# Feed forward of an encoder layer in pools left open from the second phase, with halves of whole token tiles and rows loaded part by part

## The chip, the core and the metric

The kernel runs on one core of one Trainium2 chip. The metric is the device time of one execution in microseconds (us), the median over several runs. Engines are named PE (TensorE: matmul; PEld is its weight load), DVE (VectorE), ACT (ScalarE), POOL (GpSimd) and SP (SyncE, which issues the DMAs here).

## The reference

One layer of a streaming encoder on 1024 prompt tokens and 8 × 16 = 128 sample tokens, model width 1024. All of it is computed in float32 accuracy:

```python
hq, hf, hi, hg, aq, ak, av = split_in(yp @ w_in)
mix = concat([hgrn(hq, hf, hi, hg), window_attention(aq, ak, av)]) @ w_out
mk, mv = mem_kv(mem_prompt, w_mem_kv)
x = layer_norm(ALPHA * x + mix)
x = layer_norm(ALPHA * x + mem_attention(x, mk, mv, w_mem_q, w_mem_o))
x = layer_norm(ALPHA * x + (silu(x @ w_g) * (x @ w_u)) @ w_ffn_out)
```

The sample tokens go through the same with their own caches. The change concerns the last line, called the feed forward below, whose hidden width is 2816 (22 tiles of 128, 11 pairs of tiles).

## The kernel before, in words

**Precision.** An operand in float32 is split in two: hi is a cast to fp32r (ACT, L138), lo the rest (DVE, L139); a product is three matmuls, hi·hi, lo·hi and hi·lo (all at L96). A weight tile arrives by a DMA of 512 KB into one of three raw buffers (w_raw, L149), and its halves stand in w_hi and w_lo.

**Stages.** Phase 1, to about 463 us: the combined projection, the recurrence, window attention, and the keys and values of the memory, whose copies (ACT, L269) and stores (SP, L270, L272) end it. Phase 2, 472 to 861 us: w_out, attention to the memory and its output weights, with layer norms; the rows x2 that it makes go to DRAM (x_scratch). Then the feed forward in three stages.

**Fill stage, 861 to 920 us.** The first product of the feed forward uses Strassen's form: a 2 × 2 split of weights and of x2 with seven products in place of eight. all_operands makes the seven operands of the x2 side: for each of eight token tiles, eight transposes through TensorE (L100), copies out of PSUM (ACT, L928), four subtractions (POOL, L935), seven casts (ACT, L939) and seven lo halves (DVE, one on POOL, L940). The 64 first and 64 last tokens of a tile are the two halves e. Beside it runs filler(): the gate and up products of five pairs for the 128 sample tokens, in plain float32, with weights loaded for it (L973), two sums of the PSUM bank b, and sample_gated (L961 to L964).

**Hidden stage, 920 to 1403 us.** hidden(i) makes one of 11 pairs: four weight tiles a11, a21, a22, a12 (L1004), three sums s1, s2, s4 of them (POOL, L1011 to L1013), seven products of 24 matmuls; the results are combined to m0 and m1, gated into th (L1030 to L1032), combined on POOL to the operands of the second product (t1, t2, T3 at L1067 to L1069, t4 at L1077), and stored in h_scratch (L1036). Pairs not done in the fill stage also make the sample's part (sample_pair).

**Second projection, 1403 to 1735 us.** The pairs are taken in five parts (0,2), (2,4), (4,6), (6,8), (8,11). A part multiplies the operands of two token blocks (0,1), then the sample's, then blocks (2,3); for each of seven steps operand() loads hq from h_scratch (L1161), casts hh (ACT, L1162) and takes hl (DVE or POOL, L1163). Sums go from PSUM to the rows y by add() (DVE, L1174; some through a copy and POOL, L1171 and L1172). The weights of a pair are loaded as raw2 (L1118), summed by four subtractions on POOL (L1121 to L1124), cast (ACT, L1131) and split (L1132) in prepare(i). All rows y are loaded first, as 16 DMAs of 64 rows (L1087), which take x2 back as ALPHA·x. The sample's operands hs are loaded in sample() (L1210), one buffer each. At the end final_norm writes the output, two DMAs per half row (L1089).

**What sets the order.** Each engine works through its instructions in the order in which they were written into the program; a small planner (Order) interleaves the generators by estimated TensorE time and by rank. SP's DMAs are in the same order as well, and a DMA whose buffer isn't free holds all behind it. Pools are regions of memory: closing one and opening another makes the new tiles wait for the last users of the old ones. Before, the weight pool wp is closed and opened again after phase 1, and closed with p2 before the hidden stage, where a pool f1 takes its place.

Of the kernel before, what the change touches and what calls it, by code (L numbers as in the profile page):

```python
# [9 lines left out]
F32 = mybir.dt.float32  # L10
# [23 lines left out]
FILL = 5  # L34
# [68 lines left out]
def trunk(ctx, tc, I, O):  # L103
# [12 lines left out]
    first = ctx.enter_context(ExitStack())  # L116
    cp = first.enter_context(tc.tile_pool(name="cp", bufs=1))
# [104 lines left out]
    tri = cp.tile([P, 640], U8, name="tri")  # L222
    own = cp.tile([P, 8], F32, name="own")
    sinks = cp.tile([P, 8], F32, name="sinks")
    sinks_s = cp.tile([P, 2], F32, name="sinks_s")
    gnorm = cp.tile([P, P], F32, name="gnorm")
# [3 lines left out]
    carry = cp.tile([P, HGH, P], F32, name="carry")  # L230
    V.memset(carry, 0.0)
    starts = [cp.tile([P, GW], F32, name=f"starts{i}") for i in range(2)]
# [672 lines left out]

# [16 lines left out]
    def operands(ops, j, row):  # L922

        b = {}
        st = big("stage").rearrange("p (q k e c) -> p q k e c", q=2, k=4, e=2)
        for q in range(2):
            ps = transposes(row[:, q * 512:q * 512 + 512])
            S.copy(st[:, q], ps.rearrange("p (k e c) -> p k e c", k=4, e=2))  # L928
            for e in range(2):
                b[f"B{q + 1}{e + 1}"] = st[:, q, :, e]  # L930
        tt = big("tt").rearrange("p (a k c) -> p a k c", a=4, k=4)
        for n in range(4):
            b[f"T{n + 1}"] = tt[:, n]
        for o, x, y in (("T1", "B12", "B11"), ("T2", "B22", "T1"), ("T3", "B22", "B12"), ("T4", "B21", "T2")):
            G.tensor_tensor(b[o], b[x], b[y], op=ALU.subtract)  # L935
        c = slice(j * 64, j * 64 + 64)
        for o in OPS:
            hi, lo = ops[o]
            S.copy(hi[:, :, c], b[o])  # L939
            (G if o == "T4" else V).tensor_tensor(lo[:, :, c], b[o], hi[:, :, c].bitcast(F32), op=ALU.subtract)  # L940

    def all_operands(ops, rows, ready):
        got = list(rows)

        def load(j):
            got.insert(j, big("x2_row"))
            nc.sync.dma_start(out=got[j], in_=x2_dram[TILES[j]])

        load(0)
        load(1)  # L950
        yield 3500.0
        for j in range(8):
            operands(ops, j, got[j])
            if j < 3:
                load(j + 2)
            yield 3300.0
        order.set(ready, 2000.0)
# [8 lines left out]
    def filler():  # L966

        for i in range(FILL):
            ps = [bank("b")[:, :256] for _ in range(2)]
            for e in range(2):  # L970
                for q in range(2):
                    w = raw_tile()
                    nc.sync.dma_start(out=w, in_=I["w_f1"][i, e * 2 + q])  # L973
                    for z in range(2):
                        for kt in range(4):
                            T.matmul(ps[z][:, cols(e)], w[:, cols(z * 4 + kt)], xs[:, q * 4 + kt],
                                     start=q == kt == 0, stop=q == 1 and kt == 3)
                    yield
            h = big("h_s")[:, :256].rearrange("p (e t) -> p e t", e=2)
            sample_gated(i, h, [x.rearrange("p (e t) -> p e t", e=2) for x in ps])  # L980
            yield

# [16 lines left out]
    def hidden(f1, ops, i, then):  # L999

        def wt(name, j=None):
            t = f1.tile([P, 1024], F32, name=name, tag="w", bufs=8)
            if j is not None:
                nc.sync.dma_start(out=t, in_=I["w_f1"][i, j])  # L1004
            return t

        th = [f1.tile([P, 1024], F32, name="th", bufs=2) for _ in range(2)]
        t1, t2 = (f1.tile([P, 512], F32, name=x) for x in ("t1", "t2"))
# [5 lines left out]
        m0 = [f1.tile([P, 1024], F32, name="m0", bufs=2) for _ in range(2)]  # L1014
        m1 = [f1.tile([P, 512], F32, name="m1", bufs=2) for _ in range(2)]
        t4 = f1.tile([P, 512], F32, name="t4")
# [64 lines left out]
    def out_rows(dst, b, e, row, store):  # L1081

        for n in range(2):
            at = dst[TILES[2 * b + n]][e * 64:e * 64 + 64]
            r = row[n * 64:n * 64 + 64]
            if store is None:
                nc.sync.dma_start(out=r, in_=at)  # L1087
            else:
                nc.sync.dma_start(out=at[:, store], in_=r[:, store])  # L1089

    def final_norm(y, gb, st, b, e):
# [11 lines left out]
        for hs in (h1, h0):  # L1103
            if e is None:
                nc.sync.dma_start(out=O["y"][SAMPLE][:, hs], in_=y[:, hs])
            else:
                out_rows(O["y"], b, e, y, hs)
# [42 lines left out]
    def second_projection(f2, c, ahead, prepared, prepare):  # L1150
# [54 lines left out]
        def sample(part, first, last):  # L1205
            ws = [prepared[i] for i in range(*part)]
            k = len(ws)
            for n, wk in enumerate(ws):
                q, hi, lo = (f2.tile([P, 2, P], t, name=x) for x, t in (("hs", F32), ("hsh", F32R), ("hsl", F32R)))
                nc.sync.dma_start(out=q, in_=hs_dram[:, part[0] + n])  # L1210
                split(q, hi, lo)
                for half in range(2):
                    for x in range(2):
                        mm3(sums[half], cut((hi, lo), ALL, x), wk[f"A{half + 1}{x + 1}"],
# [3 lines left out]
        prepare(PARTS[0][1], f2)  # L1218
# [3 lines left out]
        for e in range(2):  # L1222
            for b in range(4):
                out_rows(x2_dram, b, e, y[b, e], None)
        for n, part in enumerate(PARTS):
            last = n == len(PARTS) - 1
            if last:
# [5 lines left out]
            yield from sample(part, n == 0, last)  # L1233
            if last:
# [3 lines left out]
                for half in range(2):  # L1238
                    c = slice(half * 512, half * 512 + 512)
                    V.scalar_tensor_tensor(ys[:, c], ys[:, c], ALPHA, sums[half], op0=ALU.mult, op1=ALU.add)  # L1240
                    V.bn_stats(bn[:, half], ys[:, c])
# [3 lines left out]
                return  # L1245
            yield from blocks(part, (2, 3), gb)
            for _ in range(*part):
                if len(prepared) < PAIRS:
                    i = len(prepared)
                    prepare(i, f2 if i % 2 else None)  # L1250

    def feed_forward(rows):
# [3 lines left out]
        ready = Event()  # L1256
        order.add(all_operands(ops, rows, ready), 6)
        order.add(filler(), 10)
# [13 lines left out]
        for i in range(PAIRS):  # L1272
            yield from hidden(f1, ops, i, ahead if i == PAIRS - 1 else nop)
        fs.close()
# [193 lines left out]
```

## Time and profile before

| | |
|---|---|
| time, median of 3 runs | 1737.71 us (1733.31 to 1739.44) |
| the profiled execution | 1736.8 us, span 1734.9 us |
| PE busy | 1628.2 us, 94% |
| DVE, ACT, POOL busy | 1124.7, 679.9, 496.5 us |
| mean granted clock of TensorE | 0.973 |
| longest waits of PE | 22.1 us to 1425.0, 8.9 to 472.4, 5.7 to 920.1 |

A row of the waits names the engine and tile that waited, the instruction that came last, the sum, the count and the longest. A row of the timeline has start, length, engine, line, operation and count, and in brackets the idle time before and what ended it. SPq is SP's queue: its length is the time that issuing took. Granted clock 1.00 is the full clock.

### The profile page before, as it was taken

Reading aid. Unit: us, or ns where it says so; the run is one execution under the profiler, and the core shown is the slowest. Engines: PE = TensorE matmul, PEld = TensorE weight load, DVE = VectorE, ACT = ScalarE, POOL = GpSimd, SP = SyncE. Lnnn points to the kernel's source line nnn. Section 1 sums busy time; section 2 is a strip of 40 time slices with the busy share of each in tenths; the row PEclk is TensorE's granted clock in tenths of the full one; section 3 lists DMA queues with packets and bytes.
Section 4 is the critical chain, followed back from the end, with each engine's and each line's share of the span. In section 5 each row is a group of like instructions: output and inputs, shape, how many; then the busy total and the mean of one; then the engine's idle time right before and its main releaser. Section 6 shows DMA issues by size and latency. Waiting matters only on the chain.

```text
span 1734.9 us, 24529 instructions
## 1 busy us (share of the span) xinstructions
PE 1628.2 (94%) x9065; PEld 1400.6 (81%) x9065; DVE 1124.7 (65%) x2045; ACT 679.9 (39%) x1393; POOL 496.5 (29%) x401
## 2 busy tenths in 40 slices
PE   8999999999799999999978999999999948889896
PEld 7998999999688987889876888888888746667675
DVE  6886788778477666786676555444444745767576
ACT  4543456456433544225263333322222423333421
POOL 1111121111000000100075343333323535576555
PEclk9999999999999999999999999999999979999998
DMA  7453353344964588555373333322222283233353
GB/s 234 133 169 118 98 157 96 96 126 143 302 224 166 180 269 292 194 165 200 112 253 115 106 104 117 104 82 73 78 86 78 88 231 128 80 114 111 103 142 98
DMA packets 115320, 250.02 MB, mean 144 GB/s; under 512 B 12288, under 2 KB 58496, under 8 KB 115200
## 3 DMA queue, kind: packets, MB, share of 16 engines
q1 hardware_dynamic: 115200, 248.46, 44.5%
q8 instruction: 71, 1.16, 0.3%
q14 instruction: 49, 0.40, 0.1%
HBM read 205.75 MB, written 42.60 MB: 143 GB/s over the span
## 4 chain that ended last, share of the span: by engine, by line
PE 75%; DMA 8%; POOL 6%; DVE 6%; ACT 2%; issue 2%; SPq 1%; POOLq 0%; ACTq 0%; DVEq 0%
PE a L96 47%; PE b L96 20%; DMA hq<-h_scratch 3%; PE b L100 3%; PE x L96 2%; PE z L96 2%; POOL hl L1163 1%; PE s L96 1%; DVE w L1132 1%; DMA raw<-in_w_f_dram 1%; DMA y<-x_scratch 1%; DMA w_raw<-in_w_f_dram 1%; POOL s L1124 1%; DMA w_raw<-in_w_mv_dram 1%; POOL s L1123 1%
## 5 line engine op out<-in xcount | busy, mean ns | idle before, releaser
L139 DVE TENSOR_TENSOR w_lo<-w_raw,w_hi 128x1024 fp32r<-128x1024 f32 (+1 forms) x169 | 205.1, 1216 | 121.3 <-ACT w_hi L138 120.6
L138 ACT CAST w_hi<-w_raw 128x1024 fp32r<-128x1024 f32 (+1 forms) x169 | 174.6, 1035 | 200.7 <-PE a L96 82.8
L96 PE MATMUL a<-w_hi,q_hi 128*128 128x256 f32 (+1 forms) x576 | 198.9, 346 | 8.9 <-ACT w_hi L138 8.9
L96 PE MATMUL a<-w_lo,q_hi 128*128 128x256 f32 (+1 forms) x576 | 197.3, 343 | 0.0
L96 PE MATMUL a<-w_hi,q_lo 128*128 128x256 f32 (+1 forms) x576 | 196.1, 340 | 0.0
L96 PE MATMUL a<-q_hi,w_hi 128*128 128x384 f32 x528 | 187.2, 355 | 7.1 <-ACT q_hi L138 4.3
L96 PE MATMUL a<-q_lo,w_hi 128*128 128x384 f32 x528 | 180.7, 343 | 0.2 <-DVE q_lo L139 0.2
L96 PE MATMUL a<-q_hi,w_lo 128*128 128x384 f32 x528 | 180.7, 343 | 0.0
L96 PE MATMUL x<-w,hh 128*128 128x512 f32 x344 | 112.3, 408 | 40.2 <-ACT hh L1162 22.5
L96 PEld LDWEIGHTS a<-w_hi,q_hi 128*128 128x128 f32 x576 | 109.2, 190 | 22.7 <-ACT w_hi L138 9.3
L96 PEld LDWEIGHTS a<-w_lo,q_hi 128*128 128x128 f32 x576 | 109.4, 190 | 14.3 <-issue 1.2
L96 PEld LDWEIGHTS a<-w_hi,q_lo 128*128 128x128 f32 x576 | 109.3, 190 | 13.1 <-issue 0.5
L139 DVE TENSOR_TENSOR w_lo<-a,w_hi 128x1024 fp32r<-128x1024 f32 x43 | 58.4, 1359 | 88.6 <-ACT w_hi L138 88.6
L96 PEld LDWEIGHTS x<-w,hh 128*128 128x128 f32 x344 | 66.1, 195 | 59.9 <-ACT hh L1162 23.3
L96 PEld LDWEIGHTS a<-q_hi,w_hi 128*128 128x128 f32 x528 | 100.6, 190 | 12.0 <-ACT q_hi L138 4.5
L698 POOL TENSOR_TENSOR rs<-rs,mhalf 128x1 f32<-128x1 f32 x18 | 17.2, 958 | 312.6 <-DVE rs L697 312.6
L96 PE MATMUL a<-T_h,w_hi 128*128 128x512 f32 x264 | 104.3, 395 | 0.7 <-DVE m L1060 0.7
L96 PE MATMUL a<-T_h,w_lo 128*128 128x512 f32 x264 | 104.2, 395 | 0.0
L96 PE MATMUL a<-T_l,w_hi 128*128 128x512 f32 x264 | 104.2, 395 | 0.0
L96 PEld LDWEIGHTS a<-q_lo,w_hi 128*128 128x128 f32 x528 | 100.5, 190 | 2.3 <-DVE q_lo L139 1.3
L96 PEld LDWEIGHTS a<-q_hi,w_lo 128*128 128x128 f32 x528 | 100.6, 190 | 0.8 <-DVE w_lo L139 0.4
L1162 ACT CAST hh<-hq 128x512 fp32r<-128x512 f32 (+2 forms) x75 | 46.3, 619 | 106.6 <-DMA hq<-h_scratch 75.7
(305 smaller groups left out, 3957.7 us busy)
## 6 DMA issues: line engine op xcount, KB each, us to landing
a<-in_w_f_dram SPq DMA_DIRECT2D x44, 512.0 KB, 4.0
w_raw<-in_w_fm_dram SPq DMA_DIRECT2D x41, 512.0 KB, 4.1
hq<-h_scratch SPq DMA_DIRECT2D x54, 256.0 KB, 2.7
w_raw<-in_w_tm_dram SPq DMA_DIRECT2D x24, 512.0 KB, 3.5
w_raw<-in_w_out_dram SPq DMA_DIRECT2D x24, 512.0 KB, 4.8
w_raw<-in_w_mq_dram SPq DMA_DIRECT2D x24, 512.0 KB, 4.3
w_raw<-in_w_mo_dram SPq DMA_DIRECT2D x24, 512.0 KB, 4.0
h_scratch<-th SPq DMA_DIRECT2D x44, 256.0 KB, 2.2
```

Source lines behind the costliest of these rows:

```text
L96: return self.eng.matmul(out, lhsT, rhs, **kw)
L100: return self.eng.transpose(out, in_, identity)
L138: S.copy(hi, src)
L139: V.tensor_tensor(lo, src, hi.bitcast(F32), op=ALU.subtract)
L698: G.tensor_tensor(rs, rs, mhalf[:, 0:1], op=ALU.pow)
L1123: G.tensor_tensor(s4, a12, s2, op=ALU.subtract)
L1124: G.tensor_tensor(s3, a11, a21, op=ALU.subtract)
L1132: (G if name in ("A21", "A22") else V).tensor_tensor(lo, src, hi.bitcast(F32), op=ALU.subtract)
L1162: S.copy(hi, q)
L1163: (G if o in ("T1", "T3", "T4") else V).tensor_tensor(lo, q, hi.bitcast(F32), op=ALU.subtract)
```

## The change

It does the following.

1. The small constants and the recurrence's state go to the constant pool, and the state's memory (both) later serves as xs and hs. So the weight pool wp (three raw, four hi and four lo buffers) stays open from phase 1 through the hidden stage, and phase 2's pool (tiles of big(), ten buffers) through the hidden stage too.
2. FILL is 4 in place of 5, so that one more pair makes its sample's part in the hidden stage; the filler's sums are in bank a; the hidden stage waits for the filler's event.
3. operands() works on two whole token tiles j and j + 4 at a time, as halves e: four steps with tiles of 128x512, in place of eight steps with 128x256. All five rows that must be loaded are loaded first.
4. hidden() takes its tiles from big() and raw_tile(); t1 and t2 lie in m0's upper halves, t4 in m1[0].
5. The second projection's y rows are whole tiles, one DMA of 512 KB each; four are loaded ahead of the first part, four behind its blocks (0,1). The output is one DMA per half row. sample_operands loads and casts hs of all pairs of a part, in two buffers each, ahead of sample(). prepare(i) stands around sample() and blocks (2,3), and no longer behind both.

```diff
-FILL = 5
+FILL = 4
...
+            for e in range(2):
+                ps = transposes(rows[e][:, q * 512:q * 512 + 512])
+                S.copy(st[:, e], ps.rearrange("p (k c) -> p k c", k=4))
+                b[f"B{q + 1}{e + 1}"] = st[:, e]
...
-        for j in range(8):
-            operands(ops, j, got[j])
-            if j < 3:
-                load(j + 2)
-            yield 3300.0
-        order.set(ready, 2000.0)
+        for j in range(4):
+            operands(ops, j, (got[j], got[j + 4]))
+            yield 6000.0
+        order.set(ready, 1000.0)
...
-            ps = [bank("b")[:, :256] for _ in range(2)]
+            ps = [bank("a")[:, :256] for _ in range(2)]
...
+        th = [raw_tile() for _ in range(2)]
+        m1 = raw_tile()
...
+        m0 = [big("m0") for _ in range(2)]
+        t1, t2, t4 = m0[0][:, 512:], m0[1][:, 512:], m1[0]
...
-            pair = parts_of(w, *(f1.tile([P, 1024], F32R, name=x, bufs=3) for x in ("w_hi", "w_lo")))
+            pair = parts_of(w, *(wp.tile([P, 1024], F32R, name=x, bufs=N_W) for x in ("w_hi", "w_lo")))
...
+        def sample_operands(part):
+            out = []
+            for i in range(*part):
+                q, hi, lo = (f2.tile([P, 2, P], t, name=x, bufs=2) for x, t in (("hs", F32), ("hsh", F32R), ("hsl", F32R)))
+                nc.sync.dma_start(out=q, in_=hs_dram[:, i])
+                split(q, hi, lo)
+                out.append((hi, lo))
+            return out
...
-        prepare(PARTS[0][1], f2)
+        def more():
+            i = len(prepared)
+            if i < PAIRS:
+                prepare(i, f2 if i % 2 else None)
...
-        for e in range(2):
-            for b in range(4):
-                out_rows(x2_dram, b, e, y[b, e], None)
...
+            if n == 0:
+                for e in range(2):
+                    for b in range(2):
+                        nc.sync.dma_start(out=y[b, e], in_=x2_dram[TILES[b + 4 * e]])
...
             yield from blocks(part, (0, 1), gb)
-            yield from sample(part, n == 0, last)
+            hs = sample_operands(part)
+            if n == 0:
+                for e in range(2):
+                    for b in range(2, 4):
+                        nc.sync.dma_start(out=y[b, e], in_=x2_dram[TILES[b + 4 * e]])
+            while len(prepared) < min(part[1] + 1, PAIRS):
+                more()
+            yield from sample(part, hs, n == 0, last)
...
+            while len(prepared) < PARTS[n + 1][1]:
+                more()
             yield from blocks(part, (2, 3), gb)
-            for _ in range(*part):
-                if len(prepared) < PAIRS:
-                    i = len(prepared)
-                    prepare(i, f2 if i % 2 else None)
...
-        left.close()
-        fs = ExitStack()
-        f1 = fs.enter_context(tc.tile_pool(name="f1", bufs=1, reuse_waits="tile"))
+        yield filled
...
-    first.close()
-    left.close()
-    xp = ctx.enter_context(tc.tile_pool(name="xp", bufs=1, reuse_waits="tile"))
-    xs, hs = xp.tile([P, KT, P], F32, name="xs"), xp.tile([P, 256], F32, name="hs")
-    wp = left.enter_context(tc.tile_pool(name="wp", bufs=1, reuse_waits="tile"))
```

Three places in the order of the instructions. The first is SP between phases 1 and 2, before: in_w_mv are the value weights of the memory, in_w_out the first weights of phase 2, raw the operands of phase 2, kv_sb the keys and values that phase 1 stores.

```order
L149 DMA w_raw<-in_w_mv_dram 128x1024 x2
L205 DMA raw<-mix_scratch 128x384 x2
L270 DMA out_dram<-kv_sb 128x512
L272 DMA mem_kv_scratch<-kv_sb 128x256 x2
L270 DMA out_dram<-kv_sb 128x512
L272 DMA mem_kv_scratch<-kv_sb 128x256 x2
L720 DMA rows<-in_xtok_dram 128x1024 x3
L690 DMA ln_gb<-in_ln_dram 128x1024 x2
L270 DMA out_dram<-kv_sb 128x512
L272 DMA mem_kv_scratch<-kv_sb 128x256 x2
L270 DMA out_dram<-kv_sb 128x512
L149 DMA w_raw<-in_w_out_dram 128x1024 x3
```

And the same place of SP's order now:

```order
L147 DMA w_raw<-in_w_mv_dram 128x1024 x2
L147 DMA w_raw<-in_w_out_dram 128x1024
L203 DMA raw<-mix_scratch 128x384 x2
L271 DMA out_dram<-kv_sb 128x512
L273 DMA mem_kv_scratch<-kv_sb 128x256 x2
L271 DMA out_dram<-kv_sb 128x512
L273 DMA mem_kv_scratch<-kv_sb 128x256 x2
L147 DMA w_raw<-in_w_out_dram 128x1024
L721 DMA rows<-in_xtok_dram 128x1024 x3
L147 DMA w_raw<-in_w_out_dram 128x1024
L271 DMA out_dram<-kv_sb 128x512
```

The first load of in_w_out moved ahead of all stores of kv_sb, the next two between them.

The second place is POOL at the end of the hidden stage, before: the last pair's t1, t2, T3 and t4, then the subtractions s for the third prepared pair.

```order
L1067 TENSOR_TENSOR t_12813<-th 128x512
L1068 TENSOR_TENSOR t_12814<-th,t_12813 128x512
L1069 TENSOR_TENSOR th<-th 128x512
L1077 TENSOR_TENSOR t_12833<-th,t_12814 128x512
L1121 TENSOR_TENSOR s_13188<-raw_13185 128x512
```

On POOL now, where m and w_raw hold the tiles that were t and th:

```order
L1067 TENSOR_TENSOR m_12682<-w_raw 128x512
L1068 TENSOR_TENSOR m_12683<-w_raw,m_12682 128x512
L1069 TENSOR_TENSOR w_raw<-w_raw 128x512
L1111 TENSOR_TENSOR s_13205<-raw_13202 128x512
L1114 TENSOR_TENSOR s_13205<-raw_13202 128x512
L1112 TENSOR_TENSOR s_13205<-s_13205,raw_13202 128x512
L1113 TENSOR_TENSOR s_13205<-raw_13202,s_13205 128x512
L1077 TENSOR_TENSOR w_raw<-w_raw,m_12683 128x512
```

The four subtractions moved ahead of t4 (L1077).

The third place is SP at the start of the second projection, before: the store of the last t4 (h_scratch), the third pair's weights, the sample's store, the y rows, the first operands.

```order
L1036 DMA h_scratch<-t_12833 128x2x256
L1118 DMA raw_13185<-in_w_f_dram 128x1024
L964 DMA hs_scratch<-hs 128x256
L1118 DMA raw_13185<-in_w_f_dram 128x1024
L1087 DMA y<-x_scratch 64x1024 x16
L1161 DMA hq<-h_scratch 128x512 x2
L1210 DMA hs<-hs_scratch 128x256
L1118 DMA raw_13561<-in_w_f_dram 128x1024 x2
```

On SP now, from the last stores of the hidden stage on:

```order
L1036 DMA h_scratch<-w_raw 128x2x256 x3
L1227 DMA y<-x_scratch 128x1024
L962 DMA hs_scratch<-both 128x256
L1227 DMA y<-x_scratch 128x1024 x3
L1151 DMA hq<-h_scratch 128x512 x2
L1199 DMA hs<-hs_scratch 128x256 x2
L1238 DMA y<-x_scratch 128x1024
L1151 DMA hq<-h_scratch 128x512 x2
L1238 DMA y<-x_scratch 128x1024 x2
```

Four y rows stand ahead of the first hq in place of 16 half rows, the third pair's weights went ahead of the last pair's stores, and both hs of the part stand behind the first hq.

More of the change, by code (lines that the diff above doesn't have):

```diff
@@ L221, in trunk @@
     make_identity(nc, ident)
[L222 to L226, printed above, removed]
+    tri = const.tile([P, 640], U8, name="tri")
+    own = const.tile([P, 8], F32, name="own")
+    sinks = const.tile([P, 8], F32, name="sinks")
+    sinks_s = const.tile([P, 2], F32, name="sinks_s")
+    gnorm = const.tile([P, P], F32, name="gnorm")
     lb0, lb1 = (const.tile([P, 4], F32, name=f"lb{i}") for i in range(2))
@@ L229, in trunk @@
     V.memset(mhalf, -0.5)
-    carry = cp.tile([P, HGH, P], F32, name="carry")
+    both = const.tile([P, 1280], F32, name="both")
+    carry = both[:, :512].rearrange("p (h d) -> p h d", h=HGH)
     V.memset(carry, 0.0)
-    starts = [cp.tile([P, GW], F32, name=f"starts{i}") for i in range(2)]
+    starts = [both[:, 512 + i * GW:512 + (i + 1) * GW] for i in range(2)]
+    xs, hs = both[:, :1024].rearrange("p (k c) -> p k c", k=KT), both[:, 1024:]
     for t in starts:
@@ L978, in filler @@
                     yield
-            h = big("h_s")[:, :256].rearrange("p (e t) -> p e t", e=2)
+            h = hs.rearrange("p (e t) -> p e t", e=2)
             sample_gated(i, h, [x.rearrange("p (e t) -> p e t", e=2) for x in ps])
             yield
+        order.set(filled)
     def sample_pair(i, ws):
@@ L997, in parts_of, with hidden @@
         return hi, lo
-    def hidden(f1, ops, i, then):
+    def hidden(ops, i, then):
         def wt(name, j=None):
-            t = f1.tile([P, 1024], F32, name=name, tag="w", bufs=8)
+            t = big(name)
             if j is not None:
@@ L1005, in wt @@
             return t
-        th = [f1.tile([P, 1024], F32, name="th", bufs=2) for _ in range(2)]
-        t1, t2 = (f1.tile([P, 512], F32, name=x) for x in ("t1", "t2"))
+        th = [raw_tile() for _ in range(2)]
+        m1 = raw_tile()
+        m1 = [m1[:, :512], m1[:, 512:]]
         a11, a21, a22, a12 = wt("a11", 0), wt("a21", 2), wt("a22", 3), wt("a12", 1)
@@ L1079, in hidden @@
         store("T4", t4)
[L1081 to L1089, printed above, removed]
     def final_norm(y, gb, st, b, e):
@@ L1106, in final_norm @@
             else:
-                out_rows(O["y"], b, e, y, hs)
+                nc.sync.dma_start(out=O["y"][TILES[b + 4 * e]][:, hs], in_=y[:, hs])
     def second_weights(c):
@@ L1203, in blocks, with sample @@
                     yield
-        def sample(part, first, last):
+        def sample_operands(part):
[6 more added lines that the diff above has]
+            return out
+        def sample(part, hs, first, last):
             ws = [prepared[i] for i in range(*part)]
@@ L1208, in sample @@
             for n, wk in enumerate(ws):
-                q, hi, lo = (f2.tile([P, 2, P], t, name=x) for x, t in (("hs", F32), ("hsh", F32R), ("hsl", F32R)))
-                nc.sync.dma_start(out=q, in_=hs_dram[:, part[0] + n])
-                split(q, hi, lo)
                 for half in range(2):
                     for x in range(2):
-                        mm3(sums[half], cut((hi, lo), ALL, x), wk[f"A{half + 1}{x + 1}"],
+                        mm3(sums[half], cut(hs[n], ALL, x), wk[f"A{half + 1}{x + 1}"],
                             first and n == x == 0, last and n == k - 1 and x == 1, skip_group_check=True)
                 yield
-        prepare(PARTS[0][1], f2)
+        def more():
+            i = len(prepared)
+            if i < PAIRS:
+                prepare(i, f2 if i % 2 else None)
         for e in range(2):
@@ L1272, in feed_forward @@
         for i in range(PAIRS):
-            yield from hidden(f1, ops, i, ahead if i == PAIRS - 1 else nop)
-        fs.close()
+            yield from hidden(ops, i, ahead if i == PAIRS - 1 else nop)
+        left.close()
         psums.close()
```

40 lines of the change are left out of this document (16 added, 24 removed).

## The prediction

> **What bounds the kernel now.** I read the busy times first, then TensorE's waits, then its busy time and granted clock by stretch, and last the timeline at the longest waits. TensorE leads; idle elsewhere is free. The page:
>
> ```profile
> PE 1628.2 (94%) x9065; PEld 1400.6 (81%) x9065; DVE 1124.7 (65%) x2045; ACT 679.9 (39%) x1393; POOL 496.5 (29%) x401
> ```
>
> The change removes almost no matmuls, so what it can win lies in the 1734.9 − 1628.2 = 107 us in which TensorE is not busy, and in what a slow clock adds to the busy time. The waits of TensorE (in all, times, longest):
>
> ```profile
> PE x L96 <- ACT hh L1162: 22.5, 2, 22.1
> PE x L96 <- DVE y L1174: 17.7, 9, 4.0
> PE a L96 <- ACT w_hi L138: 17.5, 3, 8.9
> PE s L96 <- ACT hsh L138: 13.6, 5, 3.8
> PE b L100 <- DVE h_s L962: 3.8, 2, 2.1
> PE b L96 <- DMA w_raw<-in_w_f_dram: 3.6, 3, 1.5
> PE s L96 <- DVE hsl L139: 1.2, 2, 0.6
> ```
>
> These seven rows are 80 us, and each is a place that the diff touches. The stretches (us, then busy of PE, PEld, DVE, ACT, POOL with counts, granted clock, DMA share, GB/s): three restarts, the fill stage, and the second projection.
>
> ```profile
> 472.00:476.00 4.00, 3.57 (x8) 2.38 (x9) 3.50 (x3) 3.25 (x5) 0.00 (x0) 0.50 0.80 263
> 476.00:480.00 4.00, 4.00 (x13) 3.15 (x12) 2.34 (x4) 1.05 (x1) 0.00 (x0) 0.63 0.93 322
> 480.00:500.00 20.00, 20.00 (x88) 16.22 (x87) 13.13 (x21) 7.06 (x10) 0.00 (x0) 1.00 0.90 308
> 861.00:920.00 59.00, 44.61 (x385) 43.01 (x383) 39.13 (x66) 31.23 (x78) 34.46 (x41) 0.99 0.65 221
> 920.00:924.00 4.00, 3.82 (x8) 2.62 (x9) 1.23 (x1) 0.03 (x1) 2.02 (x1) 0.50 0.97 395
> 1425.00:1429.00 4.00, 3.96 (x9) 3.13 (x10) 2.72 (x5) 1.54 (x3) 0.94 (x1) 0.50 0.90 312
> 1449.70:1453.70 4.00, 3.97 (x16) 2.96 (x17) 0.78 (x3) 0.88 (x2) 1.29 (x1) 1.00 0.50 144
> 1478.40:1482.40 4.00, 3.98 (x11) 3.16 (x12) 4.00 (x5) 0.91 (x2) 4.00 (x3) 0.58 0.00 0
> 1482.40:1486.40 4.00, 4.00 (x19) 3.23 (x18) 4.00 (x5) 1.34 (x3) 4.00 (x3) 0.99 0.30 76
> ```
>
> A long wait is paid twice: after 472, 920 and 1425 the granted clock is 0.50. At full clock one matmul takes 20/88 = 0.227 us; the 8 + 13 after 472 took 8 us instead of 4.8, so that restart costs 3.2 more. After the 4.0 us wait that ends at 1478.41 (row below) the clock is 0.58: 11 matmuls where the next 4 us hold 19, so 4 − 11 × 0.21 = 1.7 lost. After the 2.57 us wait at 1449.71 it is 1.00.
>
> **Phase 1 to phase 2.** SP issues the first loads of the output weights behind the key and value stores, ACT casts, TensorE begins:
>
> ```profile
> 466.76 1.42 SPq L149 DMA_DIRECT2D w_raw<-in_w_out_dram  x3
> ...
> 471.29 1.04 ACT L138 CAST w_hi<-w_raw 128x1024 fp32r<-128x1024 f32 x1 [7.18 <-DMA w_raw<-in_w_out_dram]
> ...
> 472.39 1.22 PE L96 MATMUL a<-w_hi,q_hi 128*128 128x512 f32 x2 [8.90 <-ACT w_hi L138]
> ```
>
> With the weight pool left open through both phases the first of these loads follows the last value-weight load on SP and needs only an older buffer, free some 10 us before TensorE runs dry; its cast also comes before ACT's kv copies. The second and third follow within the 5 us that the first chunk lasts. The 8.9 us go, and the 3.2 behind them: −12. If the later chunks come late, up to 4 returns (bounds −8 and −12).
>
> **Fill stage.** Three groups (busy, mean ns | idle before them), then two rows of the timeline at its end:
>
> ```profile
> L96 PE MATMUL b<-xs,w_raw 128*128 128x128 f32 x320 | 38.5, 276 | 4.7 <-DMA w_raw<-in_w_f_dram 3.6 <-ACT T_h L939 1.0
> L928 ACT COPY stage<-b 128x512 f32<-128x512 f32 x16 | 8.8, 586 | 29.8 <-PE b L100 29.8
> L1069 POOL TENSOR_TENSOR th<-th 128x512 f32<-128x512 f32 x11 | 14.2, 1291 | 0.0
> 915.48 2.40 SPq L1004 DMA_DIRECT2D a<-in_w_f_dram  x5
> 920.08 0.80 PE L96 MATMUL a<-B_h,w_hi 128*128 128x512 f32 x1 [5.74 <-ACT w_hi L138]
> ```
>
> The x320 are five groups of 64 records. One group leaves: 38.5/5 = 7.7 us here, for 7.2 in the hidden stage, where a pair with the sample takes 12.74 and a plain product 5.57:
>
> ```profile
> 1085.07 5.57 PE b L96 x24
> 1124.11 12.74 PE b L96 x88
> ```
>
> The filler's sums move to the other PSUM bank, so transposes no longer wait for the gate (3.8 gone), and one fifth of the load waits goes (0.7). At the end, the loads of a11 no longer wait for the pools to close, but ACT's cast of a11 now stands behind the last step: two copies (1.2), POOL's four subtractions at 128x512 (5.2), a cast of that size (0.6, as its copy), the gate's tanh (0.4, an estimate from the copy at half the size) and the cast itself (1.04) make about 8.5 us after the first transposes. TensorE covers that with 12 more transposes and 8 matmuls in 16 records: 28 × 44.61/385 = 3.2. I take 5.3 for this gap in place of 5.74, with its half clock kept. Net: −7.7 + 7.2 − 3.8 − 0.7 − 0.4 = −5.4. The halved number of steps could also make each step's chain late (4 × 1.29 on POOL ahead of the casts): bounds +2 and −10.
>
> **Hidden stage.** Eleven pairs of the same products at 5.57. Its tiles come from the open pools; each buffer's last reader is more than 2 us ahead of its next writer by the rates above. Zero; were this wrong, each microsecond per pair costs 11.
>
> **Into the second projection.** The timeline of before there, the landing time of a store (KB, us), and the stretch of the wait:
>
> ```profile
> 1396.83 1.28 POOL L1077 TENSOR_TENSOR t<-th,t 128x512 f32<-128x512 f32 x1
> 1401.24 14.21 SPq L1087 DMA_DIRECT2D y<-x_scratch  x16
> 1416.08 1.44 SPq L1161 DMA_DIRECT2D hq<-h_scratch  x2
> 1425.04 1.22 PE L96 MATMUL x<-w,hh 128*128 128x512 f32 x2 [22.10 <-ACT hh L1162]
> h_scratch<-th SPq DMA_DIRECT2D x44, 256.0 KB, 2.2
> 1403.00:1425.00 22.00, 0.00 (x0) 0.00 (x0) 7.37 (x10) 5.17 (x9) 8.35 (x6) 0.60 1.03 263
> ```
>
> SP spends 14.2 us on 16 issues of 256 KB, and the operands hq queue behind 4.2 MB. Now four issues of 512 KB stand there, 2.1 MB; the rest comes after the first blocks. Against it: four subtractions of the next weights now precede L1077 on POOL (4 × 1.29 = 5.2), so the last hidden tile ends at 1398.1 + 5.2 = 1403.3, its store lands at 1405.5, and only then may the first y row overwrite that memory; on SP the sample's store, the other y rows and hq queue behind this wait. From 1405.5, 2.1 MB of y and 0.5 of hq take 10 us at 263 GB/s; with a cast TensorE restarts near 1416: 13 us in place of 22.1, −9. Bounds: 6 us were SP not held (−16), 22 were the loads slow again (0). The half clock stays.
>
> **Second projection.** The two sample rows above (13.6 + 1.2 = 14.8) arise thus: hs loads queue on SP behind hq loads that wait for buffers, and land as TensorE needs them.
>
> ```profile
> 1449.71 0.74 PE L96 MATMUL s<-w,hsh 128*128 128x512 f32 x2 [2.57 <-ACT hsh L138]
> 1474.88 2.88 DVE L1132 TENSOR_TENSOR w<-s,w 128x512 fp32r<-128x512 f32 x2 [2.47 <-ACT w L1131]
> 1477.69 0.67 DVE L1174 SCALAR_TENSOR_TENSOR y<-y,x 128x512 f32<-128x512 f32 x1
> 1478.41 0.73 PE L96 MATMUL x<-w,hh 128*128 128x512 f32 x2 [3.98 <-DVE y L1174]
> L1122 POOL TENSOR_TENSOR s<-s,raw 128x512 f32<-128x512 f32 x11 | 17.8, 1621 | 0.0
> raw<-in_w_f_dram SPq DMA_DIRECT2D x22, 512.0 KB, 4.3
> ```
>
> Now they are loaded in two buffers each ahead of those hq loads. The last part has three pairs for two buffers and keeps its wait, 3.8: −11 (bounds −15 and −5). At three part boundaries, DVE's y addition stood behind the next weights' subtraction, which waits for ACT, which waits for POOL; preparing elsewhere puts the additions ahead of most of that. What stood there cost 3 × (4.0 + 1.7) = 17. But one preparation per part still needs raw (4.3), a POOL subtraction (1.6) and a cast before an addition may pass, so I book only a quarter: −4.5 (bounds 0 and −15). The output in one issue per half row: nothing.
>
> **The sum.** −12 − 5.4 − 9 − 11 − 4.5 = −41.9. The profiled execution took 1736.8 us (span 1734.9), 0.9 under the median of the runs, which I leave aside: 1736.8 − 41.9 = 1695.
>
> [...] The rows show half clock after 5.7, 8.9 and 22 us of idle and none after 2.57. [...]
>
> **The rivals.** *A, the second projection gives nothing:* the moved preparations hold ACT, DVE and POOL, which work in order, at other places, and the −11 and −4.5 return: 1736.8 − 26.4 = 1710. For it: POOL's subtractions average 1.6 us there and wait for loads. Against: about 20 us of matmuls lie between a load and its use. *B, the row loads still hold TensorE:* SP waits for the late hidden store and the gap stays 22: 1704. For it, the 5.2 us on POOL; against, the halved bytes. *C, all closes:* no wait before hidden (−5.3 and its clock 3), boundaries −10 more: 1736.8 − 42 − 14 = about 1681. *D, slower:* one mechanism, at each of four parts: hh casts stand on ACT behind casts for weights not yet subtracted. A full chain for one pair is 4.3 + 4 × 1.6 + 0.6 + 1.4 (half of the x2 row at 1474.88) = 12.7, for the two pairs of a part on one POOL 19.1; with 3 for the clock, four parts lose 4 × 22.1 = 88, against 26.4 saved elsewhere and the 32 (14.8 + 17) that it replaces: 1736.8 − 58.4 + 88 = 1766. It makes the kernel slower once each part stalls by more than 58.4/4 − 3 = 11.6 us uncovered; the 20 us of cover speak against. At about that point the time would be unchanged. The edits do what they say by the instruction orders, so that they do nothing I leave within A.
>
> **How the numbers follow.** The forecast has 0.52 (its own range 1686 to 1705), A 0.21, B 0.10, C 0.09, D 0.08, of which 0.03 is near no change (0.3%, 5 us, is about what a measurement of this kernel can tell). A, B and C are faster: 0.92, 0.03, 0.05. The range, 1678 to 1718, takes in C and A with the bounds of their terms, and leaves out D and the far ends.
>
> **What would show it.** Right: no wait of TensorE over 2 us near 465 and a clock of 1.00 behind it; a wait of 4 to 6 us before the first hidden product at about 890 to 900; one of 10 to 16 before the second projection; sample waits under 5 us in all; an unchanged 5.57 per product. Wrong: boundary waits on DVE's y additions longer than 4 us, a new wait of TensorE on ACT's hh within a part, or a product above 5.6.

## The result, and the profile after

The changed kernel takes 1709.0 us (median of 4 runs, 1704.6 to 1713.8) against 1736.4 (4 runs) before: ratio 0.984, 95% interval 0.981 to 0.988, 27 us faster. The forecast was 1695 with a range of 1678 to 1718. The profiled execution took 1704.6 us (span 1702.9), 4 us less than its median, and that of before its median, so the two profiles differ by 32.

The waits of TensorE after the change, in the columns used above:

```profile
PE x L96 <- DVE y L1164: 23.6, 14, 5.6
PE x L96 <- ACT hh L1152: 15.2, 1, 15.2
PE a L96 <- ACT w_hi L136: 9.1, 2, 6.0
PE a L96 <- DVE w_lo L137: 5.4, 1, 5.4
PE z L96 <- DVE y L1164: 5.1, 4, 2.7
...
PE s L96 <- ACT hsh L136: 0.8, 1, 0.8
```

The waits on the sample's operands (14.8 before) are down to 0.8 and the 8.9 us between the phases to 0.7; the wait ahead of the second projection is 15.2 in place of 22.1. Those on DVE's y additions grew from 19.7 to 28.7, and a new one of 5.4 on DVE's w_lo stands beside that of 6.0 on w_hi. The timeline has them at the stages' starts (first the fill stage of before and of after, then the rest of after):

```profile
861.02 1.16 PE L96 MATMUL b<-xs,w_raw 128*128 128x128 f32 x9
```

```profile
845.64 2.62 PE L96 MATMUL a<-both,w_raw 128*128 128x128 f32 x22
890.53 0.80 PE L96 MATMUL a<-B_h,w_hi 128*128 128x512 f32 x1 [5.98 <-ACT w_hi L136]
897.53 0.80 PE L96 MATMUL a<-B_h,w_lo 128*128 128x512 f32 x1 [5.35 <-DVE w_lo L137]
1403.14 2.07 PE L96 MATMUL x<-w,hh 128*128 128x512 f32 x4 [15.24 <-ACT hh L1152]
```

From such starts comes this table (us; the last column runs to the span's end). The experiments stand in it too; each is described below.

| kernel | phase 1 and its wait | phase 2 | fill | hidden | wait | second |
|---|---|---|---|---|---|---|
| before | 472.4 | 388.6 | 59.1 | 482.8 | 22.1 | 309.8 |
| after | 460.0 | 385.6 | 44.9 | 497.4 | 15.2 | 299.7 |
| e1_fill_dve | 462.8 | 387.2 | 41.3 | 492.1 | 15.8 | 299.8 |
| e2_t4_first | 466.0 | 386.7 | 45.2 | 496.4 | 15.0 | 301.5 |
| e3_reopen | 468.8 | 387.7 | 45.6 | 496.7 | 14.7 | 299.2 |
| e4_prep_old | 465.9 | 386.0 | 45.3 | 496.9 | 12.9 | 295.2 |
| e5_gate_first | 462.6 | 386.7 | 47.5 | 497.5 | 8.3 | 299.5 |
| e6_spread | 460.9 | 386.1 | 47.1 | 497.5 | 12.9 | 289.0 |
| e7_hs_late | 464.2 | 386.4 | 45.5 | 496.3 | 14.9 | 309.0 |
| e8_all_three | 462.9 | 385.7 | 42.1 | 492.5 | 7.8 | 294.8 |
| e9_one_by_one | 461.1 | 385.9 | 37.4 | 493.1 | 12.3 | 293.2 |
| e10_bank_b | 461.5 | 385.9 | 48.9 | 495.0 | 15.7 | 297.2 |
| e11_fill5 | 461.9 | 385.5 | 47.0 | 496.6 | 6.0 | 299.8 |
| e12_best | 464.0 | 385.0 | 37.1 | 493.8 | 8.3 | 293.1 |

Phase 1 is the same program in all of them from "after" on, up to the pools in e3, and its end before phase 2 lies anywhere from 460.0 to 466.0, so a difference of up to 6 us in the first column is chance; the fill and hidden columns repeat within 2 or 3 us where nothing in them was edited. Between the two profiles the columns give −12.4 − 3.0 − 14.2 + 14.6 − 6.9 − 10.1 = −32.0.

### The profile page after: what moved, and what is told of

It is laid out like the page before. It is cut to its first block, busy times and chain, and to the rows that moved or that the text cites. A ratio compares the mean times of both kernels' runs of the same rounds, so it can differ in the third digit from the quotient of the medians.

```text
span 1702.9 us, 24403 instructions
## 1 busy us (share of the span) xinstructions
PE 1620.7 (95%) x9065; PEld 1391.3 (82%) x9065; DVE 1134.6 (67%) x2021; ACT 674.4 (40%) x1365; POOL 495.7 (29%) x381
## 4 chain that ended last, share of the span: by engine, by line
PE 77%; DVE 7%; DMA 6%; POOL 5%; ACT 2%; issue 2%; SPq 1%; POOLq 0%; ACTq 0%; DVEq 0%
PE a L96 48%; PE b L96 20%; PE x L96 3%; PE b L100 2%; DMA hq<-h_scratch 2%; PE z L96 1%; DVE w L1122 1%; PE s L96 1%; DMA raw<-in_w_f_dram 1%; PE w L96 1%; DVE y L1164 1%; DMA w_raw<-in_w_out_dram 1%; DMA w_raw<-in_w_fm_dram 1%; DMA w_raw<-in_w_f_dram 1%; DVE w_lo L137 1%
## 5 line engine op out<-in xcount | busy, mean ns | idle before, releaser
L137 DVE TENSOR_TENSOR w_lo<-a,w_hi 128x1024 fp32r<-128x1024 f32 x43 | 75.0, 1743 | 76.9 <-ACT w_hi L136 76.9
L96 PEld LDWEIGHTS x<-w,hh 128*128 128x128 f32 x344 | 66.6, 198 | 62.8 <-ACT hh L1152 15.7
```

The costliest lines, as they stand in the source:

```text
L96: return self.eng.matmul(out, lhsT, rhs, **kw)
L137: V.tensor_tensor(lo, src, hi.bitcast(F32), op=ALU.subtract)
```

## The experiments

All edits are made to the changed kernel. Times are medians with the ratio to before from the same chip and its interval; the changed kernel has 0.984 (0.981 to 0.988). The intervals of e2 to e6 overlap this one or touch it, so what is said of these five rests mainly on the waits and stages of one profiled execution each; e10 and e11 were run once. The edits of e1, e5 and e6 stand again in e8 and e12.

### e1: the fill stage's subtractions on DVE

```diff
-            G.tensor_tensor(b[o], b[x], b[y], op=ALU.subtract)
+            V.tensor_tensor(b[o], b[x], b[y], op=ALU.subtract)
```

> The four subtractions of each operand step go from POOL to DVE; nothing else changes. Theory 1, contention: DVE's lo halves take 1.7 us there because POOL runs its subtractions at the same time; without that they fall to 0.7 to 0.9, the two waits of TensorE around the first hidden product (6.0 and 5.4 us) fall to 6 to 8 in all, and the time falls by 4 to 6 us against the changed kernel. Theory 2, DVE simply has too much queued at that place: 16 more subtractions are 11 us more on DVE, the second wait grows beyond 5.4, and the time is 3 to 8 us more.

Measured: 1700.5 us, ratio 0.977 (0.975 to 0.980). The groups of the fill stage, in the changed kernel (busy us, mean ns of one):

```profile
L940 DVE TENSOR_TENSOR T_l<-tt,T_h 128x512 fp32r<-128x512 f32 x12 | 20.2, 1699 | 0.0
L940 DVE TENSOR_TENSOR B_l<-stage,B_h 128x512 fp32r<-128x512 f32 x12 | 14.5, 1206 | 8.1 <-ACT B_h L939 8.1
```

and in this run:

```profile
L940 DVE TENSOR_TENSOR B_l<-stage,B_h 128x512 fp32r<-128x512 f32 x12 | 9.2, 771 | 0.0
L940 DVE TENSOR_TENSOR T_l<-tt,T_h 128x512 fp32r<-128x512 f32 x12 | 7.9, 682 | 0.0
```

The same 24 subtractions take 17 us in place of 35 although DVE has 16 more instructions beside them. The timeline of the changed kernel shows the meeting one by one: 0.68 for the subtraction that begins while POOL is idle, 1.75 and 2.83 for those that begin while it works.

```profile
889.09 0.68 DVE L940 TENSOR_TENSOR B_l<-stage,B_h 128x512 fp32r<-128x512 f32 x1
889.34 1.55 POOL L940 TENSOR_TENSOR T_l<-tt,T_h 128x512 fp32r<-128x512 f32 x1 [0.73 <-ACT T_h L939]
889.69 1.75 DVE L940 TENSOR_TENSOR T_l<-tt,T_h 128x512 fp32r<-128x512 f32 x1
890.86 2.79 POOL L1011 TENSOR_TENSOR s<-a,a 128x1024 f32<-128x1024 f32 x1
891.36 2.83 DVE L940 TENSOR_TENSOR B_l<-stage,B_h 128x512 fp32r<-128x512 f32 x1
894.96 2.52 DVE L137 TENSOR_TENSOR w_lo<-a,w_hi 128x1024 fp32r<-128x1024 f32 x1
```

The subtraction of 1.75 ends 0.55 us after POOL's beside it (891.44 and 890.89), that of 2.83 ends 0.54 after POOL's (894.19 and 893.65). The same holds for all 17 of the 24 that begin while POOL works (0.55 each), and the other seven take 0.68. So the time of these 17 is not longer by a fixed factor: each lasts for the rest of POOL's instruction and 0.55.

w_lo of a11 stands behind this on DVE, and that is the wait of 5.35. In the run it is 0.84, and that on w_hi 3.94:

```profile
891.24 0.79 PE L96 MATMUL a<-B_h,w_hi 128*128 128x512 f32 x1 [3.94 <-ACT w_hi L136]
894.15 0.80 PE L96 MATMUL a<-B_h,w_lo 128*128 128x512 f32 x1 [0.84 <-DVE w_lo L137]
```

Theory 1 holds, theory 2 falls; the fill and hidden columns give 3.6 + 5.3 = 8.9 back, more than the 4 to 6 expected. With the four subtractions of each step on POOL, DVE took 35 us in place of 17 for these 24, and in the mean 1699 ns in place of 682 for the T_l among them.

### e2: t4 ahead of the weights' subtractions on POOL

```diff
+                with (tc.issue_after(ff["t4"].ins) if i == PARTS[0][1] else ExitStack()):
+                    prepare(i, f2 if i % 2 else None)
```

> POOL makes the last hidden tile t4 ahead of the four subtractions for the third prepared pair. Theory 1, the y rows' load waits for t4's store and t4 waits for POOL: the first y load is issued 4 to 5 us earlier and the wait ahead of the second projection falls from 15.2 to 10 or 11. Theory 2, the wait is set by the sample's gate and by the 2 MB of y rows in front of hq: it stays within 1 us of 15.2.

Measured: 1707.8 us, ratio 0.982 (0.980 to 0.985); the wait is 15.0. The timeline of this run:

```profile
1389.31 1.30 POOL L1077 TENSOR_TENSOR w_raw<-w_raw,m 128x512 f32<-128x512 f32 x1
1393.10 0.33 SPq L1228 DMA_DIRECT2D y<-x_scratch  x1
1398.96 0.38 ACT L959 ACTIVATE both<-b 128x256 f32<-128x256 f32 x1
1400.28 0.33 SPq L962 DMA_DIRECT2D hs_scratch<-both  x1
1400.70 1.36 SPq L1228 DMA_DIRECT2D y<-x_scratch  x3
1402.11 1.21 SPq L1151 DMA_DIRECT2D hq<-h_scratch  x2
1409.42 2.08 PE L96 MATMUL x<-w,hh 128*128 128x512 f32 x4 [15.04 <-ACT hh L1152]
```

The first y row does leave earlier, 1.3 us before TensorE runs dry where it was 4.5 behind that in the changed kernel. But the next DMA on SP is the sample's store, and it waits 7 us for the sample's gate on ACT, which stands behind the casts of the third prepared pair; the other rows and hq queue behind it. So the wait on POOL was not the last one, and theory 2 holds.

### e3: the weight pool closed and opened again after phase 1

```diff
+    left.close()
+    wp = left.enter_context(tc.tile_pool(name="wp", bufs=1, reuse_waits="tile"))
```

> The weight pool is closed and opened again after phase 1, as before, and the rest is as changed. Theory 1: the whole early gain is the load that no longer waits for the pool: a wait of about 9 us at the start of phase 2 returns with half clock behind it, and the start of the fill stage moves from 845.6 to about 858; the time rises by 12. Theory 2: the 15.4 us by which the fill stage began earlier are all of this edit: it moves to 861.

Measured: 1718.8 us, ratio 0.989 (0.986 to 0.991). A wait of 8.0 returns, phase 2 begins at 468.8 and the fill stage at 856.4:

```profile
PE a L96 <- ACT w_hi L136: 17.3, 3, 8.0
```

Against the twelve profiles of the changed kernel and the other experiments (462.8 and 386.1 on average) phase 2 begins 5.9 later and takes 1.6 more, 7.5 in all, where theory 1 had 12. By the same averages the whole early gain against before is 9.6 + 2.5 = 12.1. Where the rest of it lies is not settled by one profile, since phase 1's own end spreads over 6 us.

### e4: the weights prepared where they were before

```diff
-            while len(prepared) < min(part[1] + 1, PAIRS):
-                more()
...
-            while len(prepared) < PARTS[n + 1][1]:
-                more()
             yield from blocks(part, (2, 3), gb)
+            for _ in range(*part):
+                more()
```

(and prepare(2) ahead of part 0, as before).

> The second projection's weights are prepared where they were before (all behind blocks 2,3), the sample's operands and the y rows stay as changed. Theory 1, the moved preparations brought the 9 us of new waits on DVE's y additions (28.7 in place of 19.7): they fall to about 20, with three of 4.0, and the time falls by 5 to 9 us. Theory 2, the new waits come from the sample's operands being cast and subtracted ahead: they stay at 26 or more and the time stays within 4 us.

Measured: 1702.7 us, ratio 0.979 (0.976 to 0.981).

```profile
PE x L96 <- DVE y L1164: 22.0, 10, 4.0
PE x L96 <- ACT hh L1152: 12.9, 1, 12.9
```

With 2.3 more on the z tiles the waits on y additions are 24.3 in place of 28.7, fewer and longer, and the second projection takes 295.2 in place of 299.7. So the new placement of prepare() cost time; theory 1 has the sign and about half of the size in the waits (24.3 where it had about 20).

### e5: the sample's gate and t4 first

```diff
+                    for x in ("t4", "act", "dve") if i == PARTS[0][1] else ():
+                        st.enter_context(tc.issue_after(ff[x].ins))
```

where "act" and "dve" are the tanh and the last product of sample_gated().

> As the run with t4 first, and besides ACT's tanh and DVE's products of the last sample pair come ahead of the casts and subtractions of the third prepared pair. Theory 1, the sample's store on SP, held by its gate, holds the other y rows and hq: they are issued about 6 us earlier against the end of the hidden products and the wait ahead of the second projection falls from 15.0 to 9 or 10. Theory 2, the bytes in front of hq set it: 15 stays.

Measured: 1702.0 us, ratio 0.981 (0.978 to 0.984). Measured from where TensorE runs dry, the gate now runs 10 us sooner than in e2, and SP no longer stops between the y rows:

```profile
1388.81 0.39 ACT L959 ACTIVATE both<-b 128x256 f32<-128x256 f32 x1 [5.65 <-PE b L96]
1392.58 0.33 SPq L1230 DMA_DIRECT2D y<-x_scratch  x1
1393.00 0.38 SPq L962 DMA_DIRECT2D hs_scratch<-both  x1
1393.47 1.40 SPq L1230 DMA_DIRECT2D y<-x_scratch  x3
1394.91 1.17 SPq L1151 DMA_DIRECT2D hq<-h_scratch  x2
1402.60 2.07 PE L96 MATMUL x<-w,hh 128*128 128x512 f32 x4 [8.35 <-ACT hh L1152]
```

Theory 1 holds: 8.3. What is left is the way of hq behind 2.1 MB of y rows, 7 us from issue to cast.

### e6: one piece of a weight behind each y addition

prepare() becomes a generator with one cast and subtraction a piece:

```diff
+                    with tc.issue_after(ff["add"].ins):
+                        tick()
                     yield
```

> The weights of the second projection are cast and subtracted in single pieces, one behind each y addition, in place of all of a pair at once. Theory 1, the waits of TensorE on y additions are DVE's order alone: they fall from 28.7 us to under 8, no wait there is over 2, and the time falls by 15 to 22 us against the changed kernel. Theory 2, the chain of load, POOL and ACT is too slow for its place, wherever DVE's part stands: the waits move to later additions or to the first product that needs the late weights, and stay at 15 or more.

Measured: 1700.5 us, ratio 0.981 (0.978 to 0.983); the second projection takes 289.0 in place of 299.7. (The profile is of the fastest of its four executions; with the same order there, e8 and e12 have 294.8 and 293.1.)

```profile
PE x L96 <- DVE y L1179: 17.1, 7, 5.0
PE x L96 <- ACT hh L1167: 12.9, 1, 12.9
...
PE z L96 <- DVE y L1179: 3.4, 3, 1.8
```

The waits are 20.5 in place of 28.7, not under 8, and the time fell by 8 us in place of 15 to 22. DVE's order was a part of it, but 20.5 lies above the 15 that theory 2 named. The waits that remain show both (in e8, which has the same order there): DVE works through three pieces in a row, 1.5 us each beside POOL's work, and an hh cast comes late because hq does.

```profile
1434.01 4.57 DVE L1128 TENSOR_TENSOR w<-s,w 128x512 fp32r<-128x512 f32 x3
...
1439.08 0.62 ACT L1167 CAST hh<-hq 128x512 fp32r<-128x512 f32 x1 [4.29 <-DMA hq<-h_scratch]
```

### e7: the sample's operands loaded late again

```diff
-            hs = sample_operands(part)
...
+                q, hi, lo = (f2.tile([P, 2, P], t, name=x) for x, t in (("hs", F32), ("hsh", F32R), ("hsl", F32R)))
+                nc.sync.dma_start(out=q, in_=hs_dram[:, part[0] + n])
+                split(q, hi, lo)
```

> The sample's operands are loaded and cast in sample() with one buffer again, the rest is as changed. Theory 1, the sample's waits (14.8 us before, 1.2 now) come from this edit alone: they return to 12 to 15 and the time rises by as much. Theory 2, the moved y rows and preparations opened SP's queue: the waits stay under 6.

Measured: 1718.6 us, ratio 0.991 (0.989 to 0.993). The waits that come back are 4.4 on hsl and 1.8 on hsh, 6.2, but the stage takes 309.0, 9.3 more. The stretch of the second projection in the changed kernel, then in this run:

```profile
1403.14:1702.86 299.72, 258.23 (x1032) 199.63 (x1032) 201.03 (x287) 97.85 (x174) 176.49 (x123) 0.94 0.38 123
```

```profile
1407.31:1716.32 309.01, 264.21 (x1032) 203.15 (x1032) 200.91 (x287) 98.11 (x174) 176.97 (x123) 0.93 0.37 119
```

The same 1032 matmuls are busy 6.0 us longer, and 3.3 more is idle: between these two executions, two thirds of the difference is in TensorE's busy time, at a granted clock of 0.93 in place of 0.94. That share is not shown to hold. The mean granted clock of the four executions is 0.9775 here and 0.9788 in the changed kernel, which on 1716 us is about 2 us (an estimate) of the 9.5 between the medians. The result lies between the theories: the waits that return, 6.2, are near theory 2, and the time, 9.5, is nearer to theory 1.

### e8: e1, e5 and e6 together

> The pieces one behind each y addition, the sample's gate and t4 first, and the fill stage's subtractions on DVE, together. If the three costs are independent, as theory 1 of each says, the gains add: 9 or 10 (fill stage, as measured), 5 to 6, and 15 to 22, and the time is 1672 to 1682. If the waits only move, it stays above 1690.

Measured: 1684.4 us, ratio 0.971 (0.969 to 0.974). That is 2 above the expected range, because the range counted 15 to 22 for e6, which was still to be measured. With what the three runs gave alone, 8.5, 7.0 and 8.5 us by the medians, the sum is 1685.0: the gains add. (By the ratios, each to before on its own chip, they are 12, 6 and 7, in all 25, and 23 was measured.)

In the table the fill and hidden columns show e1's gain, the wait e5's (7.8), and the second projection 294.8, though it has e6's order and about e6's waits (21.8). Between the two profiled executions, the granted clock behind the first part's boundary makes a part of that. In e6 a wait of 5.0 ends at 1453.18, in e8 one of 3.5 at 1441.16; 2.8 us behind, e6 is back at full clock and e8 is not:

```profile
1456.00:1460.00 4.00, 4.00 (x19) 3.23 (x18) 2.66 (x4) 0.62 (x1) 3.92 (x4) 0.99 0.42 131
```

```profile
1444.00:1448.00 4.00, 4.00 (x13) 3.09 (x12) 2.03 (x3) 0.62 (x1) 3.92 (x4) 0.59 0.37 135
```

So the longer wait has the shorter stretch of half clock here. This is no cost of the combination: e8's profile is of the slowest of its four executions and e6's of the fastest, and over all four the mean granted clock is higher in e8 (0.985 and 0.978).

### e9: pieces one by one, and the operand steps closer

```diff
+                    if which != "w":
+                        with tc.issue_after(ff["add"].ins):
+                            tick()
...
+            if len(prepared) <= part[1]:
+                more()
...
-            yield 6000.0
+            yield 4500.0
```

> As the run with all three, but the pieces skip the step whose sum goes over ACT and POOL, so that no three subtractions come together on DVE, one pair of each part is prepared from the part's start, and the planner spaces the operand steps by 4.5 us in place of 6, so that 24 filler matmuls in place of 8 stand behind the last step. If DVE's order is what is left, the waits on y additions fall from 21.8 us to under 10 and the wait ahead of the first hidden product from 3.9 to under 2: 1670 to 1678. If contention between DVE and POOL alone sets them, they stay at 18 or more and the time at 1680 or more.

Both edits, and a change of the place from which a part's next pair is prepared, stand on top of e8. Measured: 1684.8 us, ratio 0.972 (0.970 to 0.974), the same as e8. The closer steps do what was expected: 24 filler matmuls cover the last chain, the fill stage falls to 37.4 and its last wait to 2.1. The rest fails: the waits on y additions are 20.8 in place of 21.8, which theory 2 had (18 or more), and the wait ahead of the second projection is back at 12.3:

```profile
PE x L96 <- DVE y L1179: 19.4, 7, 5.2
PE x L96 <- DVE w L1128: 12.3, 1, 12.3
```

The view names a weight's subtraction on DVE, which ended last, at 1389.72. But ACT's first cast of hh had ended only 0.06 us earlier, after 7.9 us of waiting for hq, so without that subtraction the wait would be as long. The cause is that of e2: ACT's casts of the third pair, now prepared earlier, stand ahead of the sample's tanh, which begins 2.3 us after TensorE ran dry (in e8 5.5 us before that), and the sample's store holds the y rows and hq on SP.

At the first boundary DVE is idle for 5.9 us: hl waits for hh, and hh's cast stands on ACT behind casts of weights whose sums POOL has not yet made. That is the order of rival D, at a quarter of its price for a part.

### e10: the filler's sums in bank b

```diff
-            ps = [bank("a")[:, :256] for _ in range(2)]
+            ps = [bank("b")[:, :256] for _ in range(2)]
```

> The changed kernel with the filler's sums in bank b again. If the transposes of the fill stage waited for the gate because of the bank, as the sum had it, its waits on the gate's DVE operation (3.8 us before) return and the stage from the first filler to the first hidden product grows from 45 to 48 or 49; if the fewer steps took them away, it stays at 45 to 46.

Measured: 1706.1 us in one run. The fill stage takes 48.9 and the waits of transposes on the gate are back with 2.9 us, in two waits (3.8 before), as the first of the two expectations has it. But the wait on w_lo is 3.0 in place of 5.4, and hidden takes 495.0. So the bank is worth about 3 us in the stage, of which about 2 go again; with one run, and fill columns from 44.9 to 47.5 where nothing in them was edited, the sizes are rough.

### e11: five filler groups

```diff
-FILL = 4
+FILL = 5
```

> The changed kernel with five filler groups again. By the sum one group is 7.7 us in the fill stage and 7.2 in the hidden stage: the fill stage grows from 45 to 52 and the hidden stage falls from 497 to 490, the total within 2. If the fifth group covers the chain at the end of the stage, the waits there (6.0 and 5.4) shrink and the total falls by 5 or more.

Measured: 1698.5 us in one run. Fill, hidden and wait are 47.0 + 496.6 + 6.0 = 549.6 in place of 557.5. The fill stage grows by only 2.1, not by 7.7, because the fifth group covers most of the chain at its end: in place of waits of 6.0 and 5.4 there is one of 3.3, and half of the group runs behind the first hidden product, where w_lo was waited for. The hidden stage falls only by 0.8 because a wait of 7.0 on the last sample pair's gate now lies inside it: the second projection's first z tile takes the PSUM that the gate still reads.

```profile
1388.10 2.90 PE L96 MATMUL z<-w,h 128*128 128x512 f32 x6 [7.04 <-DVE both L961]
```

So by the stages of this one run, four groups in place of five cost 8 us.

### e12: e8 with the closer steps

> The run with all three, and the operand steps spaced by 4.5 us. The second projection's order is that of the run with all three, since the preparation from the part's start brought the wait ahead of it back to 12.3. If the terms add, the fill stage is 37 (as measured), the wait ahead of the second projection 8, and the time 4 to 5 us under the run with all three: 1678 to 1682. If what is won in the fill stage is given back to the granted clock later, it stays at 1684.

Measured: 1679.4 us (5 runs), ratio 0.966 (0.964 to 0.969): 58 us under before on the same chip and about 30 under the changed kernel. Fill 37.1, wait 8.3, as expected, and 5 under e8: the terms add.

## Why the prediction was right or wrong, point by point

**The number.** 1709 lies outside the forecast's own range (1686 to 1705) and inside the whole one. It is 1 us from rival A's 1710, but by luck: A's reason was that the second projection gives nothing, and it gave 10. Two of the signs of being wrong came: waits on y additions longer than 4 us (5.6) and a product above 5.6 (5.62). One sum of the prediction is off by itself: rival C's terms (−5.3, −3 and −10) make 1677 and not 1681, just outside the range.

**Phase 1 to phase 2** (−12): right in size. The averages above give −12.1, the wait and the slow clock behind it. Opening the pool again alone brought 7.5 of it back (e3); what makes the other 4.6 stays open.

**Fill and hidden stage** (−5.4): wrong, +0.4. The step that failed is "I take 5.3 for this gap in place of 5.74". The gap on ACT's cast came, at 6.0, but the chain was followed on POOL and ACT alone; DVE, whose subtractions I had not followed, was the last: 1.7 us for most of them beside POOL's, and its w_lo of a11 cost 5.35 more (e1). The group that left had a cover of its own: "One group leaves: 38.5/5 = 7.7 us here, for 7.2 in the hidden stage" holds for TensorE's work, and e11 shows that the stage won only 2.1 by it. The stage without these did shrink, 59.1 to 44.9.

**Into the second projection** (−9, a wait of 13): the wait was 15.2, −6.9, right in size. That the halved bytes are part of it is likely, but no run had them whole again. The reason given for the rest was wrong: "the last hidden tile ends at 1398.1 + 5.2" was true of POOL, but e2 took that away and nothing moved. SP was held by the sample's store, and this by a gate on ACT (e5).

**Sample** (−11): right in size and in the place, with two reservations. The wait of the last part, 3.8, was to stay, and it fell as well: 14.8 came down to 0.8, and 0.8 more in the last part that the view puts down to another instruction of DVE. And the reason covers only a part: with the old loads back, 6.2 of the waits return (e7), so the rest came from the other changes to SP's queue, which no run separates.

**Part boundaries** (−4.5): wrong in sign, +9 of waits. The step that failed is "preparing elsewhere puts the additions ahead of most of that". At the four boundaries between parts it was right by half: the waits on y additions there (near 1475, 1530, 1588 and 1645 before, near 1455, 1506, 1559 and 1613 now) fell from 16.7 to 14.6. But the moved subtractions now stand ahead of additions inside the parts, where the waits grew from 3.0 to 14.1. At 1439 (a wait of 2.7) four of them stand in a row on DVE ahead of an addition. At the last boundary the chain that was to go is there in full: DVE waits for ACT's casts, which wait for POOL's sums, and the addition comes behind three subtractions.

```profile
1604.79 1.30 DVE L1122 TENSOR_TENSOR w<-raw,w 128x512 fp32r<-128x512 f32 x1 [2.07 <-ACT w L1121]
1608.47 1.08 DVE L1122 TENSOR_TENSOR w<-s,w 128x512 fp32r<-128x512 f32 x1 [2.38 <-ACT w L1121]
1611.36 1.09 DVE L1122 TENSOR_TENSOR w<-s,w 128x512 fp32r<-128x512 f32 x1 [1.80 <-ACT w L1121]
1612.37 0.67 DVE L1164 SCALAR_TENSOR_TENSOR y<-y,x 128x512 f32<-128x512 f32 x1
1613.19 1.19 PE L96 MATMUL x<-w,hh 128*128 128x512 f32 x2 [5.57 <-DVE y L1164]
```

The subtractions did not get slower: their median is 1.1 us, and 1.2 before. Rival A had this mechanism; it was true by half, since the sample's gain stayed. e4 and e6 give a part of the waits back, 4.4 and 8.2.

**The sum**: −41.9 forecast; −32.0 between the two profiles and −27 between the medians. The terms that were wrong are the fill stage (5.8) and the boundaries with their clock (about 5.4 on the second projection: −10.1 in place of −15.5), with 2.1 at the wait between; phases 1 and 2 gave 3.4 more than forecast, which by the averages above is chance. The other 5 us up to the medians are that the profiled execution of the changed kernel is the fastest of its four.

**The clock.** Half clock behind long waits was right: 0.50 again behind 890, 897 and 1403, after waits of 5.98, 5.35 and 15.24. The row behind 897:

```profile
897.50:901.50 4.00, 3.96 (x9) 3.17 (x10) 4.00 (x2) 0.00 (x0) 3.81 (x2) 0.50 0.75 264
```

But the length of one wait does not settle the clock behind it, as "none after 2.57" might suggest. The trace of before has the opposite too: behind the wait of 2.39 that ends at 1615.81, the next 4 us have 0.50. In e7 the stretch from 1510 to 1565, in which TensorE is idle for 6.7 us in all, has 0.94:

```profile
1510.00:1565.00 55.00, 48.32 (x191) 37.48 (x192) 35.98 (x46) 18.92 (x35) 32.78 (x22) 0.94 0.32 102
```

Which short waits cost the clock is not settled here: in e7 no wait for the sample's operands is over 2.0 us, and of the sample's matmuls ten records from 1486.43 take 4.04 us and ten from 1543.58 take 2.61.

## What to carry to other kernels

Follow a moved chain on every engine that has an instruction in it, and price each with what runs beside it at the new place: a DVE subtraction of 0.68 us that began while POOL subtracted ended only 0.55 us after POOL's here, and took 1.4 to 2.8. When one wait is removed, ask what the same queue waits for next; on SP one store held three loads and their readers for 7 us (e2). Work that seems to cost the same in either of two stages is worth more in the one where it covers a chain: here one filler group, by about 8 us in the one run of e11.

## What the runs showed that was not expected

A plain product of the hidden stage takes 5.62 us in the changed kernel and in every experiment on it, against 5.57 before (5.60 there once sample pairs run), about 2 us over the stage. Nothing in a product's 24 matmuls was edited but the buffers of its operands; what causes it stays open.

```profile
905.08 5.62 PE b L96 x24
```

POOL suffers too: its one subtraction per step, alone on POOL in e1 but beside a busy DVE, takes 2.6 us (1.55 in the changed kernel), while most of DVE's that follow one another beside it keep 0.68.

```profile
L940 POOL TENSOR_TENSOR T_l<-tt,T_h 128x512 fp32r<-128x512 f32 x4 | 10.5, 2616 | 29.5 <-ACT T_h L939 29.5
```
